# Ordering a kernel's instructions by another estimate of time: a transformer trunk, RWKV and S5 on one core

## The chip, the cores and the metric

The kernel runs on one core of a Trainium2 chip. The metric is device time in microseconds (us) of one execution. The engines are PE (TensorE, matrix products; PEld is its load of weights), DVE (VectorE), ACT (ScalarE), POOL (GpSimd) and SP, whose queue issues all transfers. Each engine takes the instructions of its queue in order and waits on semaphores for what other engines deliver.

## The reference

256 tokens of width 1024, with 256 tokens of context, pass two layers of a first block and one of a second, all in float32:

```
def first_block(x, c, ctx, ...):
    for l in range(2):
        mod, mod_c = silu(c) @ mod_w[l] + mod_b[l], silu(c_ctx) @ mod_w[l] + mod_b[l]
        x, xc = trunk_layer(x, xc, mod, mod_c, ...)
    return x

def trunk_layer(x, xc, mod, ...):
    z = split_columns((rmsnorm(x, pre_g) * (1 + scale) + shift) @ w_in)
    y_mla  = mla_branch(...)      # latent attention, 8 heads
    y_pool = pool_branch(...)     # mean over windows of 2, 4, 8, 16
    y_gla  = gla_branch(...)      # gated linear attention, 4 heads, both directions
    out = merge_branches(z, y_mla, y_pool, y_gla, w_branch_mla, w_branch_pool, w_branch_gla, w_out)
    return x + gate * rmsnorm(out, post_g), xc ...

def second_block(x, ...):
    proj = rms_norm(x, norm_mix_pre) @ w_in
    o_rwkv = rwkv7_branch(...) @ w_branch_rwkv
    o_s5 = s5_branch(...) @ w_branch_s5
    mixed = (g_rwkv * o_rwkv + g_s5 * o_s5) @ w_out
    x = x + rms_norm(mixed, norm_mix_post)
    return x + rms_norm(conv_ffn(rms_norm(x, norm_ffn_pre), ...), norm_ffn_post)
```

## The kernel before, in words

Features lie on the 128 partitions and tokens along the free axis: 512 columns for context and tokens together in layer 0, 256 for the tokens alone in most of layer 1 and in the second block. Weights come as units of 128x2048 in the order of use, each in two halves (`unit`, L405; seven buffers named `raw`). A half is split into a high part on ACT (`wh`, L425) and a remainder on DVE or, for every fourth, on POOL (`wl`, L427), with four buffers each; `mm3` (L435) then makes three products for each block of weights, wh by the high part of the activations, wh by their remainder, wl by the high part (L442).

The Python program writes latency-bound chains and column products interleaved by hand: `weave` (L571) emits the steps of a chain and spreads the steps of a filler over them. Layer 0 and layer 1 weave the gated linear attention (44 steps; in each of 4 heads 8 levels, `plv` products at L1113, fed by multiplications of DVE and POOL at L1104 to L1107) with merges and pooling. The norm of a head's output takes token sums (`ps_ss`, L461, of the squares of L1131), a square root of small DVE instructions (`rsqrt`, L489 to L497) and a broadcast on PE (`ps_rb`, L469). The second block weaves the RWKV chain (14 + 10 + 11 steps) with the S5 and with gates and merges; `collect`, `boundary` and `enter` make the sums and norms between blocks. Then come the feed-forward (`pup`, `pdn`) and the end.

What the program writes is not yet the order of the queues. When the tile context closes, the framework's scheduler plays the whole program on a simulated machine. Whenever an engine comes free there, it issues, of the instructions of that engine that are ready on that machine and whose buffers are free, the one that was written first. The order that results is fixed in the queues. So the estimate of durations decides where an instruction stands, but the set of instructions, their engines, buffers and transfers are those of the program. In the emitted program of the kernel before, 1822 of 8768 products on PE stand ahead of one that was written earlier, and so do 1097 of 2224 instructions on DVE, 519 of 1189 on ACT, 199 of 499 on POOL and 57 of 424 transfers on SP. At a few places the program adds an edge to hold an order (`issue_after` in `mod_chunk` and `update_x`).

Of the kernel before, what the change touches and what calls it, by code (L numbers as in the profile page):

```python
# [15 lines left out]
ALU = mybir.AluOpType  # L16
# [3 lines left out]
L = 256  # L20
# [9 lines left out]
TAU = 16.0  # L30
NSLOT = 62
MOD_AT = (0, 1, 4)     # input tiles ahead of which the next columns of the first modulation are made
S5_EARLY = 13          # state tiles of the S5 that go with the columns of the RWKV


# ---------------------------------------------------------------- host side layout
# [14 lines left out]
def _rope():  # L51
    cos, sin = _rope_tables()
    tab = np.ones((P, 2, L), np.float32)
    tab[64:96, 1], tab[96:128, 1] = cos, sin * ROPE_SIGN[:, None]
    tab[96:128, 0] = 0.0
    tab = tab.reshape(P, 2 * L)
    return np.stack([tab, np.concatenate([tab[64:], tab[:64]])])      # even heads, odd heads


class Layout:  # L60
    """Offsets of named blocks inside one [128, n] array."""
# [24 lines left out]
def _constants():  # L86
# [20 lines left out]
    sg[:64, 0], sg[64:, 0] = -1 / TAU, 1 / TAU     # decay sign of a key towards the state  # L107
    sg[:64, 1], sg[64:, 1] = 1 / TAU, 0.0
    sg[:64, 2], sg[64:, 2] = 1 / TAU, -1 / TAU     # decay sign of a query from the state
# [22 lines left out]
def _constants2():  # L132
    """tables of the second block, four [128, 512] pieces"""
# [24 lines left out]
def _w_tile(w, cols):  # L158
    """[K, len(cols)] block of w as [128, K/128 * len(cols)] (k tile major)."""
    b = w[:, cols]  # L160
    k = b.shape[0]
    return np.ascontiguousarray(b.reshape(k // P, P, -1).transpose(1, 0, 2)).reshape(P, -1)
# [18 lines left out]
def mod_columns(ch):  # L181
    """two groups of 256 columns of mod_w: chunks 0..3 shift and scale of two feature tiles, 4 and 5 halves of the gate"""
# [3 lines left out]
def host_unit(inp, key):  # L186
    """One [128, 2048] unit of the weight stream."""
# [103 lines left out]
def gate_weights(inp, l):  # L291
    """decay gates of the linear attention, on the partitions of their low-rank inputs"""
# [6 lines left out]
# ---------------------------------------------------------------- device side  # L299
# [5 lines left out]
class Halves:  # L305
    """a unit of the weight stream in two tiles, sliced like one [128, 2048]"""
# [10 lines left out]
class Arena:  # L317
    """[128, 512] slots, handed out as float32 or float32r tiles"""
# [18 lines left out]
    def cols(self, n):  # L337
        """[128, n] float32 (n = 512 or 256); two of 256 share a slot"""
# [21 lines left out]
class B:  # L360
# [43 lines left out]
    # -- weights  # L404
# [16 lines left out]
    def split(self, src, n, pool=False):  # L421
        """exact high part and remainder of a [128, n] block of weights"""
# [12 lines left out]
    def mm3(self, ps, w, xs, cols, off=0, m=P, start=True, stop=True):  # L435
        """ps += W.T @ X over len(xs) contraction tiles, with split operands"""
# [8 lines left out]
    # -- small helpers  # L445
    def after(self, ts, value):
        """[128, 1] constant that exists once the (finite) tiles ts do: keeps activations of one table together"""
# [7 lines left out]
    def token_sums(self, ps, c0, *accs, f=None):  # L455
        """ps[:, c0 + t] = f * sum over the partitions of token tile t of accs; returns the next column"""
# [8 lines left out]
    def bcast(self, r, n, pool):  # L465
        """PSUM [128, 128 n]: per-token columns r spread over all partitions"""
# [10 lines left out]
    def rstd(self, acc, dim, pool):  # L477
        """PSUM broadcast of 1/sqrt(mean + eps) from sums of squares that are still spread over partitions"""
# [4 lines left out]
    def rsqrt(self, m, n):  # L483
        """m ** -0.5 of a small tile: bit estimate, then a second- and a third-order step"""
# [7 lines left out]
        nc.vector.scalar_tensor_tensor(r, t, -3.0, r, ALU.add, ALU.mult)      # -2 times the second estimate  # L492
# [7 lines left out]
    # -- residual stream: x += out * rstd(out), then the next block's normalised input  # L500
    def collect(self, st, ps, gain, xs, nxt=True):
        """take one output tile: keep it times its gain and add up the sums the norms need"""
# [26 lines left out]
        if k == 6:  # L529
            # the sums of all tiles but the last, ahead of it  # L530
# [11 lines left out]
    def boundary(self, st, A, n, nxt=True):  # L542
        """PSUM broadcasts of rstd(out) and of rstd(x + out * rstd(out)); A: mean square of x per token, plus eps"""
# [27 lines left out]
def weave(chain, nc_, filler, nf):  # L571
    """emit a latency-bound chain (nc_ steps) with filler work (nf steps) spread over it"""
# [9 lines left out]
def mix(a, c):  # L582
    """step two generators in turn until the first ends, then finish the second"""
# [7 lines left out]
def mod_chunk(b, l, ch, ahead=False, between=None):  # L591
    """mod_columns(ch) of silu(c) @ mod_w + mod_b for (c_ctx, c)"""
# [35 lines left out]
def build_h(b, k, xs, seqs, gain, shift, pr2, hi_, lo_):  # L628
    """normalised (and modulated) input tile k, as its high part and remainder"""
# [15 lines left out]
def update_x(b, k, st, xs, s_, pr, rs, on_pool):  # L645
    """x += out * rstd; rs: copy of pr in SBUF, for the tiles of the engine that can't read PSUM"""
# [12 lines left out]
def enter(b, st, xs, s_, A, h, gain, shift, pool):  # L659
    """residual of one sequence, then its normalised input of the next block into h, tile after tile"""  # L660
# [11 lines left out]
def trunk(b, l, xs, st, A):  # L672
    """one layer of the first block; st: output tiles of the layer before that x still lacks"""
# [3 lines left out]
    QC = ALLC if full else XC          # columns that get an output  # L677
# [5 lines left out]
    # ---- pre norm, and the first columns as its tiles come  # L683
# [94 lines left out]
    def mla_prep():  # L778
# [12 lines left out]
        # rotary keys for the cosine and the sine part of the queries, on the lower and the upper partitions  # L791
# [25 lines left out]
    def parts(t):  # L817
        """a [128, 512] slot as its high part and remainder, in two new ones"""
# [5 lines left out]
    # ---- attention  # L824
# [40 lines left out]
    def pair_values(hd, prs, vt, py):  # L865
        """both heads of a pair, one product of each in turn: they fall on different columns of the array"""
# [23 lines left out]
    def silu2(ps):  # L890
        """2 * silu of a PSUM tile"""
# [1180 lines left out]
```

## Time and profile before

| | |
|---|---|
| median of 3 runs | 1586.6 us (1584.66 to 1589.52) |
| span of the profiled execution | 1585.3 us |
| its time with what lies around the span | not shown apart; span and median differ by 1.3 us |
| PE, PEld, DVE, ACT, POOL busy | 91%, 78%, 70%, 43%, 31% |
| moved from and to HBM | 188.19 MB, 119 GB/s on the mean |

An engine's busy time is the time that its instructions cover. Products on PE overlap each other, so a busy PE isn't one at its peak; idle time is what lies between. The granted clock of PE is a mean over its two levels, 1.00 for 2.4 GHz throughout and 0.50 for 1.2 GHz.

### The profile page before, as it was taken

The numbers are of one execution on the slowest core, as the hardware profiler recorded it, in microseconds if no ns is written. First come the engines' busy times: TensorE is split into PE (matmuls) and PEld (weight loads), VectorE is DVE, ScalarE is ACT, GpSimd is POOL, SyncE is SP. The second block draws the span as 40 slices with busy tenths as digits, with TensorE's granted clock in tenths as the row PEclk, the third lists the DMA queues.
The fourth block names the chain that finished last, engine by engine and source line by source line (L and its number), as shares of the span: only waits on it lengthen the run. The fifth ranks groups of instructions, "written<-read, shape, count | busy, mean of one in ns | idle before, by whom it ended". The sixth has DMA issues, their size and how long they took to land. (4 is left out here: it accounts for less than half of the span.)

```text
span 1585.3 us, 26747 instructions
## 1 busy us (share of the span) xinstructions
PE 1448.5 (91%) x10316; PEld 1232.7 (78%) x10316; DVE 1116.2 (70%) x2224; ACT 684.7 (43%) x1251; POOL 490.5 (31%) x503
## 2 busy tenths in 40 slices
PE   5999999998999999899988899979879999699997
PEld 2676766876788778886777799867548998699996
DVE  4565558886768655865599977779987348888843
ACT  3434445333323334354554445532343235366642
POOL 1000013353335954410134421436541002521212
PEclk8999999999999999899999999979989999799999
DMA  9634421221133262234033245834103224356550
GB/s 354 206 115 150 134 93 40 92 71 51 55 94 110 76 224 88 94 107 160 27 91 109 81 136 171 272 100 127 51 24 94 69 81 145 95 174 188 184 182 32
DMA packets 61183, 188.19 MB, mean 119 GB/s; under 512 B 7040, under 2 KB 8448, under 8 KB 61056
## 3 DMA queue, kind: packets, MB, share of 16 engines
q1 hardware_dynamic: 61056, 186.49, 36.7%
q8 instruction: 81, 1.33, 0.3%
q14 instruction: 46, 0.38, 0.1%
HBM read 180.43 MB, written 6.03 MB: 118 GB/s over the span
## 5 line engine op out<-in xcount | busy, mean ns | idle before, releaser
L425 ACT CAST wh<-raw 128x1024 fp32r<-128x1024 f32 (+1 forms) x296 | 279.6, 949 | 308.0 <-issue 64.5
L427 DVE TENSOR_TENSOR wl<-raw,wh 128x1024 fp32r<-128x1024 f32 (+1 forms) x225 | 271.2, 1208 | 162.8 <-ACT wh L425 159.8
L427 POOL TENSOR_TENSOR wl<-raw,wh 128x1024 fp32r<-128x1024 f32 (+1 forms) x71 | 144.2, 2032 | 649.0 <-ACT wh L425 600.1
L442 PE MATMUL z_merge<-s,wh 128*128 128x512 f32 (+1 forms) x768 | 198.7, 347 | 1.3 <-ACT s L940 1.3
L442 PEld LDWEIGHTS z_merge<-s,wh 128*128 128x128 f32 x768 | 134.0, 194 | 17.7 <-issue 2.0
L442 PE MATMUL z_merge<-s,wl 128*128 128x512 f32 (+1 forms) x384 | 131.8, 343 | 2.2 <-DVE wl L427 2.1
L442 PE MATMUL pbr<-s,wh 128*128 128x256 f32 (+1 forms) x512 | 120.2, 325 | 3.5 <-ACT s L432 2.4
L442 PE MATMUL pup<-s,wh 128*128 128x256 f32 x656 | 118.5, 283 | 0.1
L442 PEld LDWEIGHTS pup<-s,wh 128*128 128x128 f32 x656 | 102.5, 192 | 0.2 <-ACT wh L425 0.2
L442 PE MATMUL y<-s,wh 128*128 128x256 f32 x496 | 98.7, 294 | 0.0
L442 PE MATMUL pwo<-s,wh 128*128 128x256 f32 (+1 forms) x448 | 95.3, 310 | 2.7 <-ACT s L1220 2.0
L442 PEld LDWEIGHTS pbr<-s,wh 128*128 128x128 f32 x512 | 86.2, 191 | 12.8 <-ACT s L432 3.0
L442 PE MATMUL pup<-s,wl 128*128 128x256 f32 x328 | 92.8, 283 | 0.0
L442 PEld LDWEIGHTS z_merge<-s,wl 128*128 128x128 f32 x384 | 74.5, 194 | 11.5 <-DVE wl L427 3.2
L442 PE MATMUL pbr<-s,wl 128*128 128x256 f32 (+1 forms) x256 | 83.1, 325 | 0.0
L442 PEld LDWEIGHTS y<-s,wh 128*128 128x128 f32 x496 | 78.6, 193 | 5.8 <-issue 3.5
L442 PEld LDWEIGHTS pwo<-s,wh 128*128 128x128 f32 x448 | 76.0, 202 | 6.6 <-ACT s L1220 2.6
L1102 ACT ACTIVATE s<-s 128x512 f32<-128x512 f32 (+1 forms) x64 | 33.1, 523 | 97.2 <-DVE s L1101 92.6
L442 PE MATMUL y<-s,wl 128*128 128x256 f32 x248 | 71.6, 289 | 2.2 <-DVE wl L427 2.2
L432 ACT CAST s<-s 128x256 fp32r<-128x256 f32 (+1 forms) x88 | 42.8, 488 | 69.1 <-DVE s L1175 19.6
L442 PE MATMUL pwo<-s,wl 128*128 128x256 f32 (+1 forms) x224 | 69.0, 308 | 1.5 <-DVE wl L427 1.5
L1113 PE MATMUL plv<-s,s 128*128 128x128 f32 x384 | 53.9, 284 | 14.4 <-POOL s L1105 8.2
(478 smaller groups left out, 3684.9 us busy)
## 6 DMA issues: line engine op xcount, KB each, us to landing
raw<-wts SPq DMA_DIRECT2D x294, 512.0 KB, 4.3
s<-wts SPq DMA_DIRECT2D x57, 256.0 KB, 5.4
s5t<-s SPq DMA_DIRECT2D x16, 256.0 KB, 2.0
s<-s5t SPq DMA_DIRECT2D x16, 256.0 KB, 3.4
s<-xc SPq DMA_DIRECT2D x8, 256.0 KB, 4.0
x<-xc SPq DMA_DIRECT2D x8, 256.0 KB, 4.8
s<-tabs SPq DMA_DIRECT2D x4, 256.0 KB, 4.6
out<-s SPq DMA_DIRECT2D x8, 128.0 KB, 1.8
```

Source lines behind the costliest of these rows:

```text
L425: self.nc.scalar.copy(hi[:, :n], src)
L427: self.last_lo = eng.tensor_sub(lo[:, :n], src, hi[:, :n])
L432: self.nc.scalar.copy(hi, src)
L442: self.nc.tensor.matmul(ps, u, v[:, cols], start=start and n == 0, stop=stop and n == last)
L1102: nc.scalar.activation(E[:, lo:], E[:, lo:], AF.Exp, scale=1.0 / TAU)
L1113: nc.tensor.matmul(ps[:, c], K_[:, j], Z[:, c], start=True, stop=True)
```

## The change

The tile context gets the flag by which the scheduler plays the program on the framework's timeline simulation, with that simulation's durations, instead of on its plain estimate. All else of the program is the same; the other lines of the diff take comments away and leave the line numbers.

```
--- before.py
+++ after.py
@@ -2057,7 +2057,7 @@
     ap["wts"] = nc.dram_tensor("wts", (n_units, P, UNIT), F32, kind="ExternalInput").ap()
     ap["out"] = nc.dram_tensor("out", (8, P, L), F32, kind="ExternalOutput").ap()
-    with tile.TileContext(nc) as tc:
+    with tile.TileContext(nc, schedule_with_timeline_sim=True) as tc:
         b = build(tc, ap, lay)
         assert len(b.order) == n_units, len(b.order)
```

## Rows read from the trace of the kernel before

**Rows 1.** The page: busy us, share of the span, instructions of three engines.

```profile
PE 1448.5 (91%) x10316; PEld 1232.7 (78%) x10316; DVE 1116.2 (70%) x2224; ACT 684.7 (43%) x1251; POOL 490.5 (31%) x503
```

**Rows 2.** Busy time by stage: stretch, length, engines, granted clock, DMA share, GB/s.

```profile
0.00:40.00 40.00, 23.21 (x78) 8.72 (x81) 18.70 (x46) 14.44 (x28) 5.13 (x6) 0.83 0.96 351
40.00:240.00 200.00, 196.45 (x1062) 137.79 (x1062) 113.19 (x336) 87.30 (x180) 13.41 (x13) 1.00 0.42 138
240.00:600.00 360.00, 338.62 (x1647) 276.84 (x1646) 268.36 (x448) 134.31 (x213) 175.17 (x199) 0.99 0.29 93
600.00:800.00 200.00, 186.58 (x1214) 156.69 (x1213) 129.17 (x302) 92.09 (x188) 50.99 (x57) 0.95 0.28 91
800.00:920.00 120.00, 100.38 (x729) 94.88 (x728) 112.31 (x286) 61.76 (x125) 51.90 (x73) 0.93 0.31 93
920.00:1000.00 80.00, 80.00 (x661) 79.80 (x660) 56.13 (x99) 38.89 (x65) 14.58 (x14) 0.98 0.55 173
1000.00:1043.00 43.00, 31.10 (x217) 29.72 (x216) 31.32 (x57) 18.41 (x36) 25.12 (x25) 0.79 0.68 224
1043.00:1200.00 157.00, 135.63 (x997) 102.65 (x998) 140.13 (x220) 63.38 (x118) 74.71 (x66) 0.92 0.23 73
1200.00:1320.00 120.00, 117.12 (x1802) 109.07 (x1797) 59.12 (x123) 37.45 (x75) 8.78 (x6) 0.99 0.28 85
1320.00:1393.00 73.00, 58.81 (x438) 56.69 (x436) 60.19 (x112) 34.96 (x67) 28.14 (x27) 0.86 0.39 116
1393.00:1573.00 180.00, 179.56 (x1493) 179.10 (x1492) 120.36 (x182) 101.21 (x160) 39.38 (x16) 1.00 0.52 161
1573.00:1585.30 12.30, 1.01 (x6) 0.71 (x6) 7.27 (x23) 0.48 (x2) 3.17 (x4) 0.70 0.25 85
```

**Rows 3.** Waits of PE from 240 to 600: total us, times, longest.

```profile
PE plv L1113 <- POOL s L1105: 8.2, 5, 2.2
...
PE z_merge L442 <- DVE wl L427: 2.1, 1, 2.1
PE pbr L442 <- ACT s L432: 2.0, 1, 2.0
PE ps_ss L461 <- ACT s L1131: 1.8, 1, 1.8
```

**Rows 4.** Instructions in order of time around 379 us: start, duration, engine.

```profile
377.64 0.42 DVE L1106 TENSOR_TENSOR s<-s,s 64x256 f32<-64x256 f32 x1
377.65 1.11 POOL L1104 TENSOR_TENSOR s<-s,s 64x256 f32<-64x256 f32 x1 [2.44 <-ACT s L1102]
...
378.10 0.94 DVE L1107 TENSOR_TENSOR s<-s,s 64x256 f32<-64x256 f32 x1
378.72 1.01 POOL L1105 TENSOR_TENSOR s<-s,s 64x256 f32<-64x256 f32 x1
...
379.78 1.16 PE L1113 MATMUL plv<-s,s 128*128 128x128 f32 x8 [1.71 <-POOL s L1105]
...
383.60 0.71 PE L442 MATMUL z_pool_gate<-s,wh 128*128 128x512 f32 x2
```

**Rows 5.** The same view from 1102 to 1112 us, DVE, then PE.

```profile
1102.56 1.21 DVE L427 TENSOR_TENSOR wl<-raw,wh 128x1024 fp32r<-128x1024 f32 x1
1103.69 0.17 DVE L490 TENSOR_TENSOR t<-r 128x16 f32<-128x16 f32 x1
1103.78 0.68 DVE L1551 TENSOR_TENSOR s<-bu,s 128x512 f32<-128x512 f32 x1
...
1109.18 1.17 DVE L497 SCALAR_TENSOR_TENSOR r<-u,r 128x16 f32<-128x16 f32 x1
...
1111.10 1.46 PE L1532 MATMUL py<-s,s 128*32 128x256 f32 x3 [3.11 <-DVE rnk L1635]
```

**Rows 6.** The chain that ended last: the feed-forward's first product.

```profile
1393.17 115.42 PE pup L442 x960
```

More of the change, by code (lines that the diff above doesn't have):

```diff
@@ L2059, in make @@
     ap["out"] = nc.dram_tensor("out", (8, P, L), F32, kind="ExternalOutput").ap()
-    with tile.TileContext(nc) as tc:
+    with tile.TileContext(nc, schedule_with_timeline_sim=True) as tc:
         b = build(tc, ap, lay)
```

## The prediction

> **What bounds the kernel now.** I read four views: the shares of the engines, the busy time by stage, the waits of the matrix engine, and the order of time around a few of its gaps.
>
> The shares say that the matrix engine (PE) leads with 1448.5 us of a span of 1585.3, before DVE with 1116.2 and POOL with 490.5 [rows 1]. So an order of instructions can win back only the 1585.3 - 1448.5 = 136.8 us in which PE is idle, and what a low clock costs in its busy time. The stages show where these lie [rows 2]. Idle time is the length less PE's busy time; clock loss is the length times what the granted clock lacks to 1.00 (a mean over 1.2 and 2.4 GHz).
>
> - 0 to 40: 16.8 idle, while the DMA engines are busy for 0.96 of the time: the first weights arrive.
> - 40 to 240, 920 to 1000, 1200 to 1320: 3.6, 0 and 2.9 idle. Nearly full.
> - 240 to 600 (attention chain of layer 0): 21.4 idle, 3.6 of clock.
> - 600 to 800 (end of layer 0, start of layer 1): 13.4 and 10.0.
> - 800 to 920 (the same chain in layer 1): 19.6 and 8.4; DVE is busy for 112.3 of 120 us.
> - 1000 to 1043 and 1320 to 1393: 11.9 and 14.2, the two block boundaries.
> - 1043 to 1200 (RWKV chain and S5): 21.4 and 12.6; DVE is busy for 140.1 of 157.
> - from 1393: 11.7 idle, all but 0.4 of it in the last 12 us; before that 960 products of the feed-forward follow each other in 115.42 us [rows 6], 0.120 us each, with no gap to fill.
>
> **The change part by part.** It removes and adds no instruction, transfer or byte. It replaces the estimate by which the scheduler decides what is ready when an engine comes free. The queues run in order, so a wrong estimate costs in two ways: an instruction stands too early and its engine waits in front of ready work, or ready work of lesser urgency goes first and the chain waits.
>
> The first kind is in the trace. At 379.78 PE has waited 1.71 us for POOL's product of L1105, which took 1.01 us after one of 1.11 [rows 4]; the column products behind it start at 383.60 without a wait. The order before treats POOL as if it were done by then. Between 240 and 600 such waits for POOL come to 8.2 us, and 1.8 more for the square of L1131 [rows 3]. The waits of 2.1 and 2.0 us for a weight split and for the inputs of the merge [rows 3] have no other work behind them and stay.
>
> The second kind is there too: in the square root of the RWKV norms every small DVE instruction stands behind a large one, 0.17 us (L490) after a split of 1.21, and so on to L497 at 1109.18; PE then waits 3.11 us [rows 5]. An order by another estimate can mend this or spread it.
>
> An estimate nearer to the chip should mostly shorten waits of the first kind. No row shows the new order, so each stage is bounded by nothing gained and by all of its idle and clock time:
>
> - 240 to 600: waits with work behind them 8.2 + 1.8 = 10.0, clock 3.6. Two thirds of the first and half of the second: 9 us (bounds 0 and 13.6). I take most here because DVE is busy for only 268 of 360 us, so PE sets the end of the stage.
> - 600 to 800: a third of 13.4 + 10.0: 8 us (0 and 23.4). DVE at 129 of 200 leaves room, but part of this is the boundary between the layers, with little to put in.
> - 800 to 920: a quarter of 28.0: 7 us (0 and 28.0). DVE at 94% is nearly a second bound; work pulled into a gap is missing at the end of the stage, where PE then waits for the chain.
> - 1043 to 1200: an eighth of 34.0: 4 us (0 and 34.0), for the same reason.
> - Beginning, two boundaries and end: 0. Their 54.6 us of idle are a transfer or chains of sums and norms with no columns left; the order among a few dependent instructions has nothing to exchange.
> - Feed-forward and 920 to 1000: 0. PE is full, and its columns depend on nothing late.
>
> That is 28 us. Against it stand the stages where the present order leaves PE hardly idle. 40 to 240 and 1200 to 1320 mix chains with columns as 240 to 600 does, and idle 6.4 us of 320; at the rate of 240 to 600, 21.4 of 360, it would be 19.0. A new order can only lose here, 0 to 12.6 us. I take two thirds, 8, since nothing says that the new order hits the same lucky places. SP's queue moves too, in the sense that its loads are ordered by the same estimate: the 16.8 us at the start bound it, and elsewhere the DMA engines are at most 0.68 busy [rows 2], so I cost it at 0; were that cover gone, a late load would hold a split and then PE, as at the start.
>
> **A rule against the change.** DVE and POOL lengthen each other: L1106 on DVE took 0.42 us as POOL's L1104 began, and the like-shaped L1107, wholly beside it and its successor, 0.94 [rows 4]. A better packed order has more such pairs. 64 levels run in the attention chains (2 layers of 4 heads of 8 levels). One more lengthened DVE instruction in each costs 0.5 us in layer 0 and, on half the columns, 0.25 in layer 1: 16 + 8 = 24 us, of which only the 8 of layer 1 surely reach the end, since DVE has 92 us free between 240 and 600. The Trainium skill, "GPSIMD Engine Reference", section Key points, states that GpSimd shares its SBUF interfaces with VectorE and contends with instructions that have two SBUF inputs, and the trace agrees (0.42 against 0.94). By the page alone the sum would lose these 8 to 24 us; I leave them out of the sum, because the pairs exist already and a new order may have fewer, and keep them as a rival.
>
> **The sum.** 28 - 8 = 20 us less. The profiled execution has a span of 1585.3 us, 1.3 below the median of 1586.6 and inside the runs shown (1584.66 to 1589.52); what lies around the span isn't shown apart, and I carry the 1.3 over. 1585.3 + 1.3 - 20 = 1566.6, so 1567.
>
> **The rivals.**
>
> *The chains swallow it.* Where DVE is busy for 94 and 89%, filling PE's gaps only moves the idle time to the end of the stage, and 600 to 800 is boundary. Then 9 us are won and 8 lost: 1586. For it: DVE's two near-full stages hold half of the idle time that order could reach. Against it: in 240 to 600 PE is the later one.
>
> *Fillers overtake the chains (slower).* Place: DVE's queue from 800 to 920 and 1043 to 1200, with 44 steps of one chain and 35 of the other as the kernel weaves them. Price: a weight split of 1.21 us [rows 5] started just before a chain instruction is ready delays it by half on the mean, 0.6. Half of the 79 steps hit cost 24 us; the 11 us of these stages aren't won, so 9 + 8 - 8 = 9 remain as gain: 1586.6 + 24 - 9 = 1602. It decides from 15 steps on (9 / 0.6). For it: rows 5 show the pattern already, and the order before puts chains early, which costs PE but protects them. Against it: a split that goes early isn't there later, and a chain that PE no longer blocks starts sooner.
>
> *Closer pairing of DVE and POOL*, as above: 1567 + 8 to 24, 1575 to 1591, middle 1583.
>
> *Larger gain.* Half of all that order could reach: (13.6 + 23.4 + 28.0 + 34.0) / 2 = 49.5, nothing lost: 1537. For it: most of those waits have columns behind them. Against it: DVE's share.
>
> The change does nothing at all only if both estimates agree on every choice; rows 4 show the old one off by more than a microsecond, so I give that no chance of its own.
>
> **How the numbers follow.** Forecast 0.48 (own range 1547 to 1583: 28 us give or take 12, the loss between 0 and 12.6), swallowed 0.16, overtaken 0.22, pairing 0.06, larger 0.08. A measurement of this kernel tells 0.3%, 4.8 us, from no change: faster is below 1581.8, slower above 1591.4. Faster: 0.47 of the forecast and 0.08, 0.55. Same: swallowed and the rest of the forecast, 0.17. Slower: overtaken, and pairing as far as losses join it, 0.28. The range must take in both signs: 1540 leaves out half of the larger gain (0.04), 1610 the worse third of overtaken (two thirds of the 79 steps cost 32 us: 1610) and a little else, 0.10.
>
> **What the new profile would show.** Right: PE's busy share above 91%; waits of L1113 for POOL under 4 us in the attention stage of layer 0; that stage shorter by some 9 us and the one after it by some 8; the feed-forward still at 0.120 us a product, the boundaries still with 12 and 14 us idle. Swallowed: the waits for POOL gone, but the stage as long, with a wait at its end. Overtaken: fewer waits of PE in the middle of columns, but long ones for DVE, and splits ahead of small instructions on DVE. Pairing: the mean duration of the same DVE instructions up. I'd be wrong altogether if new gaps opened in the stages that are now full, or if loads of weights came late.

## The result and the profile after

The changed kernel took 1644.45 us in the median (1643.18 to 1645.43), the kernel before beside it 1585.84 (1584.66 to 1589.52): a ratio of 1.0367, 95% interval 1.0344 to 1.0390. It is slower by 58 us; the prediction was faster by 20. The instructions are the same; only their order in the five queues differs.

The page of the profile after, with the busy time of the engines, answers to [rows 1]:

```profile
PE 1457.9 (89%) x10316; PEld 1238.5 (75%) x10316; DVE 1121.7 (68%) x2224; ACT 683.9 (42%) x1251; POOL 506.4 (31%) x503
```

The span is 1642.8 us, so PE is idle for 184.9 us where it was idle for 136.8. The mean granted clock fell from 0.956 to 0.937 of full speed (a mean over 1.2 and 2.4 GHz): 1642.8 x 0.063 = 103.5 us lost, 1585.3 x 0.044 = 69.8 before. But for part of the time at the low clock PE is idle anyway, and that part must not be counted twice. Counted along the clock records of the trace, with half of the busy time at 1.2 GHz as lost, the low clock takes 67.2 us out of PE's busy time, 51.4 before. What is left, PE's work at full clock, went down from 1397.1 to 1390.7. So idle time added 48.1 us, the clock 15.8, and shorter work took 6.4 away: 57.5 in all, the difference of the spans.

Busy time by stage, to be set against [rows 2]. The borders are put by the same products: the first `pgate` product, where the linear attention starts, moved from 239 to 280, the first `pwo` from 586 to 608, the last `pgate` from 798 to 843, the first of the second block from 1042 to 1081.

```profile
40.00:281.00 241.00, 218.65 (x1122) 153.85 (x1121) 114.88 (x342) 91.61 (x184) 13.53 (x13) 0.95 0.35 116
281.00:621.00 340.00, 324.90 (x1606) 267.62 (x1606) 274.81 (x447) 131.95 (x210) 185.15 (x200) 0.99 0.29 92
621.00:846.00 225.00, 197.79 (x1305) 165.92 (x1305) 133.42 (x308) 97.52 (x195) 51.73 (x58) 0.92 0.27 91
846.00:1038.00 192.00, 166.89 (x1294) 160.67 (x1293) 165.64 (x377) 94.68 (x182) 66.69 (x86) 0.95 0.40 126
1038.00:1082.00 44.00, 29.18 (x216) 27.92 (x215) 33.49 (x64) 17.74 (x37) 26.74 (x25) 0.80 0.64 225
1082.00:1255.00 173.00, 150.00 (x1074) 115.04 (x1074) 146.51 (x223) 65.60 (x121) 79.15 (x66) 0.86 0.26 79
1255.00:1371.00 116.00, 110.07 (x1736) 103.43 (x1735) 49.92 (x109) 33.99 (x69) 6.42 (x5) 0.93 0.23 71
1371.00:1451.00 80.00, 58.12 (x421) 54.73 (x421) 59.92 (x117) 34.91 (x67) 30.71 (x27) 0.85 0.32 100
```

Worked out as in the prediction (idle is length less PE's busy time, the clock's loss is length times what the clock, rounded to two digits, lacks to 1.00); the column after it is the loss in PE's busy time alone, from the clock records:

| stage (before) | length | PE idle | lost to the clock | in busy time alone | forecast |
|---|---|---|---|---|---|
| 40 to 240, latent attention of layer 0 | 200 -> 241 | 3.6 -> 22.4 | 0 -> 12.1 | 0 -> 10.6 | part of +8 |
| 240 to 600, linear attention of layer 0 | 360 -> 340 | 21.4 -> 15.1 | 3.6 -> 3.4 | 5.1 -> 1.7 | -9 |
| 600 to 800, with the latent attention of layer 1 | 200 -> 225 | 13.4 -> 27.2 | 10.0 -> 18.0 | 9.9 -> 13.7 | -8 |
| 800 to 1000, linear attention of layer 1 | 200 -> 192 | 19.6 -> 25.1 | 10.0 -> 9.6 | 9.9 -> 6.6 | -7 |
| 1043 to 1200, RWKV and S5 | 157 -> 173 | 21.4 -> 23.0 | 12.6 -> 24.2 | 9.2 -> 15.9 | -4 |
| 1200 to 1320, RWKV and merges | 120 -> 116 | 2.9 -> 5.9 | 1.2 -> 8.1 | 1.7 -> 7.6 | part of +8 |
| 1320 to 1393, boundary | 73 -> 80 | 14.2 -> 21.9 | 10.2 -> 12.0 | 5.4 -> 4.9 | 0 |

A stage can also grow or shrink because columns are done ahead of it; the experiments take that apart. Two terms came as forecast. The feed-forward's products follow each other as in [rows 6]:

```profile
1450.90 115.42 PE pup L442 x960
```

And PE no longer waits for POOL in the linear attention of layer 0. These waits of PE from 280 to 608 are all there are in the place of [rows 3]:

```profile
PE plv L1113 <- DVE s L1116: 5.6, 7, 1.4
PE pst L1075 <- ACT s L1073: 3.3, 1, 3.3
PE pbr L442 <- ACT s L432: 2.0, 1, 2.0
PE ps_rb L469 <- DVE r L497: 1.5, 1, 1.5
PE po L1125 <- DVE s L1116: 1.4, 2, 0.9
PE plv L1113 <- DVE s L1107: 0.8, 1, 0.8
PE pst L1072 <- DVE s L1068: 0.3, 1, 0.3
```

**Where the loss begins.** In the latent attention a chain (`mla_chain`, L911) makes for each of 8 heads the keys and queries (`pk`, `pq`), the scores (`psc`, L851), their softmax on DVE and ACT (L853 to L858), the transposes (`ptr`, L876) and the values (`py`, L883). It is woven at L1206 with filler columns that don't depend on it: the gates, the first columns of the linear attention (`pgv`, L1016) and the next modulations (`pmod`, L606). PE's waits from 105 to 280 in the kernel after:

```profile
PE psc L851 <- ACT s L432: 5.8, 4, 3.0
PE psc L851 <- ACT s L856: 5.7, 4, 1.4
PE ptr L876 <- ACT s L856: 3.5, 5, 1.7
PE pq L442 <- ACT s L856: 1.7, 1, 1.7
PE pmod L614 <- ACT s L612: 1.1, 2, 0.7
PE psc L851 <- DVE s L433: 1.1, 2, 0.6
```

In the same stage of the kernel before, PE waited 0.8 us for the scores' operands, once, and 0.7 for others. One such place in the changed kernel, in order of time (start, duration; in brackets PE's or ACT's idle time and what ended it):

```profile
156.56 0.28 PE L1016 MATMUL pgv<-wl,s 128*128 128x256 f32 x1
...
165.46 1.66 PE L442 MATMUL pq<-s,s 128*128 128x512 f32 x6
168.46 1.04 ACT L425 CAST wh<-raw 128x1024 fp32r<-128x1024 f32 x1 [0.93 <-DMA raw<-wts]
170.08 0.90 PE L851 MATMUL psc<-s,s 128*128 128x256 f32 x4 [2.95 <-ACT s L432]
...
173.76 2.91 PE L851 MATMUL psc<-s,s 128*128 128x512 f32 x6
176.47 0.63 PE L1016 MATMUL pgv<-wh,s 128*128 128x256 f32 x2
```

Between the query and the scores PE has nothing else to do: the last column product ended at 156.8 and a modulation at 163, and the weights of the next columns have only arrived at 168.46. Their loads had waited for a buffer that a modulation product on PE still had to read, as the longest of the waits of SP's queue from 140 to 175 shows:

```profile
SPq L410 <- PE pmod L606: 21.6, 1, 21.6
```

In the kernel before, such products of a query and its scores had column products between them (a query at 121.77, columns from 123.28 on, the scores at 124.89). The busy time of the stretches around the place shows that the clock falls too; the number after the engines is the granted clock:

```profile
140.00:160.00 20.00, 16.44 (x107) 12.68 (x107) 8.86 (x29) 8.41 (x20) 0.00 (x0) 1.00 0.39 141
160.00:180.00 20.00, 16.61 (x85) 11.57 (x83) 10.04 (x27) 8.65 (x18) 2.52 (x1) 0.83 0.47 157
180.00:200.00 20.00, 16.74 (x81) 11.55 (x84) 6.05 (x18) 7.44 (x18) 0.00 (x0) 0.74 0.00 1
```

PE idles for 3.6 us in the first stretch at full clock, and then runs at a mean of 0.83 and 0.74. The six score products above took 2.91 us; the like six took 1.66 in the kernel before.

How far the fillers run ahead can be counted along PE's instructions in their order: the filler products that stand ahead of the first score product of each head of layer 0.

| head | 1 | 2 | 3 | 4 | 5 | 6 | 7 | 8 |
|---|---|---|---|---|---|---|---|---|
| before | 101 | 130 | 165 | 207 | 265 | 301 | 353 | 408 |
| after | 148 | 196 | 232 | 260 | 348 | 400 | 404 | 408 |

There are 408, so the last three heads have almost none left. From these rows came the first theory: the fillers overtake the chain in PE's queue, which costs the 62 us by which the two latent-attention stages grew up to their `pgate` products (in layer 0 139.4 to 175.0 us from 100 and 105 on, in layer 1 119.3 to 145.8 from the last `z_misc` product on). The rivals: the weight loads come late; or the queues of DVE and ACT hold the chain up.

### The profile page after: what moved, and what is told of

Same layout as the page of the kernel before. It is cut to its first block, busy times and chain, and to the rows that moved or that the text cites. A ratio compares the mean times of both kernels' runs of the same rounds, so it can differ in the third digit from the quotient of the medians.

```text
span 1642.8 us, 26795 instructions
## 1 busy us (share of the span) xinstructions
PE 1457.9 (89%) x10316; PEld 1238.5 (75%) x10316; DVE 1121.7 (68%) x2224; ACT 683.9 (42%) x1251; POOL 506.4 (31%) x503
## 4 chain that ended last, share of the span: by engine, by line
PE 40%; DVE 12%; issue 2%; ACT 2%; POOL 1%; DMA 1%; DVEq 0%; ACTq 0%; POOLq 0%
PE pup L442 7%; PE y L442 5%; PE pdn L442 4%; PE z_merge L442 3%; PE pbr L442 3%; DVE wl L427 2%; PE py L1532 2%; PE pgv L1016 1%; PE pwo L442 1%; PE pen L442 1%; DVE s L1520 1%; PE py L883 1%; DMA raw<-wts 1%; PE z_mla_gate L442 1%; PE z_gla_gate L442 1%
## 5 line engine op out<-in xcount | busy, mean ns | idle before, releaser
L427 POOL TENSOR_TENSOR wl<-raw,wh 128x1024 fp32r<-128x1024 f32 (+1 forms) x71 | 148.8, 2097 | 740.9 <-ACT wh L425 662.2
L442 PE MATMUL z_merge<-s,wh 128*128 128x512 f32 (+1 forms) x768 | 194.8, 341 | 2.4 <-ACT s L940 1.3
L442 PE MATMUL pbr<-s,wh 128*128 128x256 f32 (+1 forms) x512 | 125.7, 332 | 3.5 <-ACT s L432 2.0
L442 PE MATMUL pwo<-s,wh 128*128 128x256 f32 (+1 forms) x448 | 89.6, 299 | 0.0
L433 DVE TENSOR_TENSOR s<-s,s 128x256 fp32r<-128x256 f32 (+1 forms) x88 | 51.9, 593 | 37.3 <-ACT s L432 34.7
L442 PEld LDWEIGHTS pwo<-s,wh 128*128 128x128 f32 x448 | 72.0, 191 | 2.6
L1113 PE MATMUL plv<-s,s 128*128 128x128 f32 x384 | 56.8, 290 | 18.9 <-DVE s L1116 12.0
L1113 PEld LDWEIGHTS plv<-s,s 128*128 128x128 f32 x384 | 51.2, 200 | 25.9 <-issue 16.1
```

The source lines that it names most:

```text
L427: self.last_lo = eng.tensor_sub(lo[:, :n], src, hi[:, :n])
L433: self.nc.vector.tensor_sub(lo, src, hi)
L442: self.nc.tensor.matmul(ps, u, v[:, cols], start=start and n == 0, stop=stop and n == last)
L1113: nc.tensor.matmul(ps[:, c], K_[:, j], Z[:, c], start=True, stop=True)
```

## The experiments

### Whose order is it?

An order can be copied. Every instruction has the same name in both kernels, so a list of names in the order of one kernel, with an edge from each to the next that fixes the order in the queue and waits for nothing, gives a chosen queue in a chosen stage of the other kernel that order (the edits are shown in outline here and below):

```diff
         b = build(tc, ap, lay)
+        for names in ORDERS.values():     # per engine, in the order to be copied
+            for last, name in zip(names, names[1:]):
+                tc.add_manual_dep(named[name], last, edge)   # order alone, no wait
```

What is on no list is left to the scheduler. **pe_order_old** lists PE in the two latent-attention stages.

> The changed kernel, with one thing put back: in the two latent-attention stages the matrix engine's queue has the order that it had before the change; the other queues and all other stages stay with the timeline estimate. Theory (on PE's queue the filler columns overtake the attention chain, so that the chain is late and its end has no columns left): the 62 us by which the two stages grew (35.6 and 26.5) come back for the most part, 1575 to 1605 us, and PE's idle time and its low clock in them go. Rival 1 (weights arrive late because the load queue was reordered): no more than 10 us come back, above 1630. Rival 2 (DVE's and ACT's queues hold the chain up): half or less, above 1610.

1617.2 us, ratio to before 1.0198 (1.0180 to 1.0216): 27 us came back, not 40 to 70. That lies outside the theory's bounds and inside those of rival 2, which the next run tests.

**dve_act_order_old** lists DVE, ACT and POOL there instead.

> The changed kernel, with DVE's, ACT's and POOL's queues in the two latent-attention stages in the order before the change, PE's and the load queue free. Rival 2 (those queues hold the chain up): 1575 to 1605. Theory (PE's queue does it): these queues alone bring back less than half of the 62 us, 1610 to 1650, since PE still sends the fillers ahead of the chain (196 filler products lie ahead of the second head's first score product, 130 in the kernel before; here 172).

1655.9 us, 1.0443 (1.0424 to 1.0462): nothing came back; it is 12 us slower than the changed kernel.

**load_order_old** lists SP's queue, in the whole program.

> The changed kernel, with the load queue of the whole program in the order before the change and all else free. Rival 1 (late loads): 1600 or less. Theory: no change, 1638 to 1650, since a load waits for its buffer, and the buffers are freed by PE's and DVE's order.

1652.9 us, 1.0429 (1.0413 to 1.0444): nothing came back, 8 us slower. So the order of the loads isn't what makes the weights late; at the place above they waited for a buffer that PE had to free.

**pe_order_new_alone** is the reverse, in the kernel before.

> The reverse, in the kernel before: only PE's queue in the two latent-attention stages gets the order of the changed kernel, all else goes by the plain estimate. Theory (that order alone makes the loss): 40 to 65 us more than before, 1626 to 1651. If the loss needs the other queues too (rival 2) or the loads (rival 1): less than 20 us more, below 1606.

1621.4 us, 1.0235 (1.0216 to 1.0253): 35 us lost by PE's order in these two stages alone, a little less than the theory's least. Where, the starts of the same products show. The last column before the forms is first and last start, of the kernel before and of this one:

```profile
L1027 PE MATMUL pgate<-s,s x16: 587/587/692, 239.4 to 797.7; 32*128 32x512 f32 x16
L442 PE MATMUL pwo<-s,wh x448: 277/283/561, 586.5 to 1360.0; 128*128 128x256 f32 x128, 128*128 128x512 f32 x22
L442 PE MATMUL pup<-s,wh x656: 280/283/415, 1380.0 to 1508.2; 128*128 128x256 f32 x164
```

```profile
L1027 PE MATMUL pgate<-s,s x16: 587/587/692, 267.8 to 836.3; 32*128 32x512 f32 x16
L442 PE MATMUL pwo<-s,wh x448: 277/283/561, 612.8 to 1393.3; 128*128 128x256 f32 x128, 128*128 128x512 f32 x22
L442 PE MATMUL pup<-s,wh x656: 280/283/415, 1413.3 to 1541.2; 128*128 128x256 f32 x164
```

28.4 us are lost by the first `pgate`, 26.3 by the first `pwo` of layer 0, 38.6 by the last `pgate`, 33.3 by the feed-forward; nothing is lost after the stages whose order was changed.

**mla_all_old** lists all five queues in the two stages.

> The changed kernel, with all five queues in the two latent-attention stages in the order before the change. If PE's order alone matters there: as with PE's alone, 1613 to 1620. If the other queues' orders matter together with PE's: 5 to 20 us less, 1597 to 1612; what is left above 1586 is then the RWKV stage's loss (19 us) less the gain in the linear-attention stages.

1615.6 us, 1.0182 (1.0167 to 1.0197): as with PE's alone. In these stages the order of the other queues adds nothing to that of PE, which is worth 27 us taken back and 35 put in. The theory had the right queue and stage and half the size: the 62 us were measured up to the `pgate` products, and part of them was work done ahead. With all five old orders the first `pgate` still starts at 263.6, 24.2 later than before, but the first `pwo` at 591.1, only 4.6 later. 29 us stand elsewhere.

### Is it the lead of the fillers?

**fillers_held** keeps the timeline estimate and holds the fillers by the step:

```diff
     for _ in chain:
         i += 1
+        ends.append(last PE product traced so far)
+        with b.tc.issue_after(ends[-2]):       # from the second step on
             while done * nc_ < i * nf and next(filler, 1) is None:
                 done += 1
```

> The changed kernel, with a rule in place of a copied order: in the two latent-attention stages the PE products of a filler step are queued behind the last PE product of the chain step before the one after which they are written, so a filler can be at most about one step ahead. Theory (it is the lead of the fillers over the chain that costs, not this or that detail of the order): as much comes back as with PE's whole old order, 20 to 35 us, 1610 to 1625. Rival (other details of PE's order make the loss): less than 10 us back, above 1635.

1637.3 us, 1.0318 (1.0301 to 1.0336): 7 us back, within the rival's bounds. The filler products ahead of the heads' first scores are now 108, 132, 168, 180, 240, 288, 348 and 360, fewer than before the change from the fourth head on, and still PE waits. The largest of its waits from 104 to 269 in this kernel (total, times, longest):

```profile
PE psc L859 <- ACT s L864: 13.1, 8, 3.0
```

(L859 and L864 are L851 and L856.) The lead is gone from the fourth head on and the loss in layer 0 is not: the first `pwo` starts at 607.2, in the changed kernel at 607.7.

**fillers_rationed** spreads them: filler product n goes behind the chain product at the same share of the chain as product n - 60 has of the fillers (never behind one that is written after it); **fillers_rationed_40** and **fillers_rationed_80** change the 60.

```diff
+        for n, ins in enumerate(filler products):
+            m = (n - 60) * len(chain products) // len(filler products)
+            tc.add_manual_dep(ins, chain products[m], edge)
```

> The changed kernel, with the filler products of the two latent-attention stages rationed on PE: product n of the fillers is queued behind the chain product that stands at the same share of the chain as product n - 60 does of the fillers, so the stock is spread over the chain's waits and no step can use it up in its first wait. Theory (holding fillers by the step gave nothing back in layer 0 since a step's stock is spent in its first wait; spread, it covers all waits): as with PE's old order, 15 to 30 us less than the changed kernel, 1614 to 1630. Rival (some other detail of PE's old order is what counts): less than 8 us, above 1636.

1628.9 us, 1.0268 (1.0240 to 1.0295): 15 us back.

> fillers_rationed with an allowance of 40 products in place of 60. Theory (spreading the fillers over the chain's waits gives back part of what PE's order cost): 10 us or more under the changed kernel, below 1634. Rival (the 15 us that came back with 60 are scatter, since any change of the order moves the time by some 10 us either way, as it did for the loads' order, +8, and the late fillers, +12): anywhere within 8 us of the changed kernel, 1636 to 1652.

1639.9 us, 1.0328 (1.0303 to 1.0353): 5 us back, within the rival's bounds.

> fillers_rationed with an allowance of 80. Theory: less than with 60 comes back, 4 to 16 us, 1628 to 1640. Rival (scatter): as likely slower as faster than the changed kernel.

1631.2 us, 1.0278 (1.0252 to 1.0304): 13 us back.

**chain_24_forward** leaves the fillers in their lumps and moves the chain up:

```diff
+        for each chain product: ahead = max(ahead - 24, fillers written before it)
```

> The changed kernel, PE's queue in the two latent-attention stages in its own new order, but with each chain product moved up past as many as 24 filler products that were written after it; the fillers keep their lumps. If the lead as such costs: 8 us or more come back, below 1636. If it matters how the fillers lie among the chain's waits, and not how far ahead they are: within 8 us of the changed kernel, 1636 to 1652.

1646.8 us, 1.0381 (1.0355 to 1.0408): no change. This run alone is a weak test, since the lead of the changed kernel over the one before is 47 to 99 products for the first seven heads, and 24 take away only part of it.

So the lead as such, held in fillers_held and cut in chain_24_forward, doesn't explain the loss. A ration, which is meant to put a few filler products into each wait, gave 5, 15 and 13 us back, always with the sign of the theory and never the 27 of the old order; with orders that were expected to change nothing or to help (loads, and DVE with ACT and POOL) moving the time by 8 and 12 us, only part of this is safe. That the fillers must lie between the chain's waits is supported, not shown; what makes the rest of the 27 us stays open.

**fillers_early** and **fillers_early_half** go the other way, in the kernel before with its plain estimate:

```diff
+        with b.tc.high_priority(240):          # 120 in fillers_early_half, -80 in fillers_late
             while done * nc_ < i * nf and next(filler, 1) is None:
```

> The kernel before with its plain estimate, where the filler steps of the two latent-attention stages are given the priority of instructions written 240 places earlier, so that they run as far ahead of the chain as in the changed kernel (196, 260, 400, 408 filler products ahead of the first score products of heads 2, 4, 6 and 8 of layer 0; 130, 207, 301, 408 in the kernel before). Theory (the lead costs): 25 to 45 us more than before, 1611 to 1631, as with the copied order of PE. Rival (the timeline estimate's order is bad for another reason): within 10 us of before, below 1596.

1666.8 us, 1.0508 (1.0486 to 1.0530): 80 us lost, more than expected. PE idles 39.3 us longer than before (1665.3 - 1489.2 = 176.1), the clock takes 19.3 more of its busy time, and the work at full clock is 21.4 longer.

> As fillers_early, the plain estimate with the fillers of the two latent-attention stages written early, but by 120 places and not 240 (169, 260, 338, 408 filler products ahead of the first score products of heads 2, 4, 6 and 8; 130, 207, 301, 408 before, 196, 260, 400, 408 with 240, which cost 80 us). Theory (the loss grows with the lead, and faster once the stock runs out): 10 to 40 us more than before, 1597 to 1627. Rival (the loss is all in the start, where fillers pushed the chain back by 27 us): proportional there alone, under 10 us, below 1597.

1615.0 us, 1.0180 (1.0150 to 1.0210): 29 us lost, as expected, but not in the way expected: PE's busy time is 1476.9 of a span of 1616.2 at a mean clock of 0.954, so it idles for 139.3 us, hardly more than the 136.8 before. The work itself is longer by 26.0 us, and the last section shows the most of why. So of these two only the first bears the theory out, and a quarter of its loss (21.4 of 80) is longer work.

> The kernel before with its plain estimate, the filler steps of the two latent-attention stages written 80 places later (57, 151, 238, 355 filler products ahead of the first score products of heads 2, 4, 6 and 8; 130, 207, 301, 408 before). Theory (only fillers that run ahead cost): within 8 us of before, 1579 to 1595, since fillers that are left over are done in the next stage. Rival (the order before is a point to which the steps were fitted, and any departure from it costs): 12 us more or over, above 1599.

1598.1 us, 1.0073 (1.0047 to 1.0099), 12 us more, between the two bounds. PE idles less than before (1597.6 - 1465.9 = 131.7), its work is longer by 15.2. So late fillers don't make PE wait, but this departure from the old order costs too, by the same lengthening of the work.

### The other half

**rwkv_new_alone**: all queues listed in the old order up to the second block, free under the timeline estimate from there.

> The timeline estimate with all queues in the old order up to the start of the second block, and free from there. If the RWKV stage's loss stands by itself: 14 to 24 us over before, 1600 to 1611, and then the loss of the change is the sum of this, of the 33 to 35 us of PE's order in the latent-attention stages and of about nothing elsewhere. Rival (it comes with the state that the first block leaves in the queues): below 1595.

1607.4 us, 1.0129 (1.0098 to 1.0159): 20 us (16 to 25) lost in the second block alone. The busy times by part, first of the kernel before and then of this one, cut at the start of the block, the last input product of the S5 (`bu`) and at the end of the RWKV's first score products (`sc`):

```profile
1042.00:1153.00 111.00, 101.20 (x640) 77.47 (x640) 99.46 (x153) 43.28 (x76) 56.76 (x51) 0.94 0.30 93
1153.00:1197.00 44.00, 32.10 (x296) 23.06 (x297) 38.68 (x63) 18.56 (x40) 18.88 (x17) 0.84 0.06 17
1197.00:1380.00 183.00, 166.05 (x2205) 156.07 (x2201) 113.49 (x221) 68.77 (x135) 36.69 (x32) 0.94 0.34 104
```

```profile
1045.00:1143.00 98.00, 92.11 (x614) 72.28 (x616) 89.39 (x132) 35.80 (x62) 51.79 (x44) 0.97 0.33 104
1143.00:1211.00 68.00, 50.03 (x426) 37.41 (x424) 54.85 (x88) 30.11 (x61) 28.27 (x23) 0.80 0.16 48
1211.00:1394.00 183.00, 155.73 (x2101) 145.91 (x2097) 105.33 (x216) 63.52 (x127) 36.20 (x31) 0.91 0.30 91
```

The S5, which is the filler there, ends 13 us sooner, and the stretch from there to the end of the first score products takes 24 us longer, with 18.0 us idle for 11.9 and a clock of 0.80 for 0.84. But 130 more products run in it, most of them taken from the third stretch, which then idles for 27.3 us for 17.0 at the same length. So the block loses idle time after the S5's end and more of it later on; which instruction stands wrong is not shown. The profiled execution is the fastest of its four, and its block is only 11 us longer.

**rwkv_dve_old** (DVE's queue of the second block in the old order, all else of the changed kernel) and **pe_order_old_and_rwkv** (pe_order_old, with PE's queue of the weaves at L1934 to L1937 as well) ask which queue it is.

> The changed kernel, with DVE's queue in the second block up to the feed-forward's start (RWKV chain, S5, merges) in the order before the change, all else free. Theory (there the S5's instructions overtake the RWKV chain in DVE's queue: 59 of them lie ahead of the first broadcast of the key norms, 39 before the change): 10 to 20 us come back, 1624 to 1634. Rival (the loss there is on PE, or comes with the state that the first block leaves): less than 5 us, above 1639.

1644.4 us, 1.0360 (1.0342 to 1.0378): no change.

> pe_order_old with PE's queue in the RWKV stage's weaves (RWKV chain, S5, merges) in the old order as well. If the RWKV stage's loss of 17 us is PE's order too: 1598 to 1606. If it is not (DVE's order alone gave nothing back): 1612 to 1622.

1633.4 us, 1.0294 (1.0266 to 1.0323): 16 us slower than without it. Neither of these two old orders mends it, and an old order in one queue beside new ones in the others can do harm of its own.

**rwkv_fillers_early** puts the fillers of the four weaves 80 places earlier, under the plain estimate.

> The kernel before with its plain estimate, the filler steps of the second block's four weaves (S5 steps, merge columns) written 80 places earlier. PE's queue then has 60 S5 products ahead of the first broadcast of the key norms and 444 merge products ahead of the last (44 and 407 before; 61 and 444 in the changed kernel). Theory (the same mechanism as in the latent-attention stages): 12 to 50 us more than before, 1599 to 1637, lost from the S5's end on. Rival (the RWKV stage loses in another way): below 1595.

1761.6 us, 1.1119 (1.1075 to 1.1163): 176 us, far outside, and by another mechanism (last section).

**timeline_for_gla_only** lists all queues in the old order except from the linear attention to the end of each layer.

> The timeline estimate with all queues in the old order everywhere but from the linear-attention stage of each layer to the layer's end, so that the estimate is free only where the trace seemed to show a gain (the stage was 19 us shorter in layer 0 and 7 in layer 1). If that gain is real: 1565 to 1580, better than both kernels. If it was only columns done ahead in the stage before it: 1582 to 1592, no change.

1589.8 us, 1.0021 (1.0006 to 1.0036): no gain that lasts. The first `pwo` starts at 581.2, 5.3 us sooner than before, and the first product of the second block at 1042.5, 0.2 later. Layer 0 gains and layer 1 gives it back.

Where the loss stands, the starts of the same products show (first `pwo` in layer 0, first `bu` in the second block, first `pup` of the feed-forward, from their tiles' views):

| | first `pwo` | first `bu` | first `pup` |
|---|---|---|---|
| before | 586.5 | 1060.1 | 1380.0 |
| after | 607.7 | 1097.5 | 1438.1 |
| mla_all_old | 591.1 | 1069.0 | 1407.9 |
| pe_order_new_alone | 612.8 | 1093.2 | 1413.3 |
| rwkv_new_alone | 589.9 | 1061.0 | 1394.4 |

The change loses 37.4 us up to the first `bu`, and the old orders of the latent attention bring 28.5 of them back; it loses 20.7 us from there to the first `pup`, and they change that little (19.0). Put into the kernel before, the parts are 35 us (PE's order in the latent attention), 20 (second block) and 3 (linear attention to the end of the layers), 58 together; that this meets the whole so closely is in part luck, since PE's order gave back only 27 when it was taken out. No kernel that ran beat the one before.

## Why the prediction was wrong

- **PE bounds the kernel, and order can only move its idle time and clock.** PE leads after the change too. But the prediction read the bound in one direction: 136.8 us to win. Nothing bounds the loss, since an order can make idle time where there was none.
- **Waits for POOL go (right).** 8.2 us before, no row after. In their place stand 5.6 us for L1116 on DVE.
- **240 to 600 gains 9 us (mechanism right, size off).** The stage is 20 us shorter, but 13.7 of it are PE's busy time for 41 products fewer, done outside the stage; idle time fell by 6.3. By itself (timeline_for_gla_only) the new order there gained 5 us by the first `pwo`, and they were lost again by the second block.
- **800 to 920 gains 7 (wrong).** Shorter by 8 with the columns after it, but its idle time rose (19.6 to 25.1), and in timeline_for_gla_only layer 1 lost what layer 0 had won.
- **The step that failed: "A new order can only lose here, 0 to 12.6 us", put at 8.** The nearly full stages were priced at the idle rate of another stage. Instead, PE's new order in the two latent-attention stages cost 35 us by itself (pe_order_new_alone). In the changed kernel PE's idle time rose by 18.8 us in 40 to 240, and by another 13.8 in 600 to 800, which holds the latent attention of layer 1 and was counted as a gain of 8. The idle rate of 240 to 600 is no bound for a stage with other waits: there are eight heads here, each with a softmax between two groups of products, and PE's waits in the first of the two stages rose from 1.5 us to 18.9. The prediction named the sign itself ("if new gaps opened in the stages that are now full") and gave it no price beyond 12.6.
- **What the clock adds.** The prediction counted the clock as something to win, never as a price of a new order. Up to the first `bu` this matters little: 35.7 us more of idle time, 2.5 of clock in busy time, 0.8 less work make the 37.4. From there to the first `pup` it is the larger part: 12.1 of idle time, 13.9 of clock, 5.3 less work make the 20.7.
- **1043 to 1200 gains 4 (wrong).** The second block alone lost 20 (rwkv_new_alone). It stays open which queue does it.
- **SP's queue costs nothing (right as far as tried).** Its old order gave nothing back. The boundary put at 0 at 1320 was not: it idles 7.7 us longer.
- **The rival that came nearest** was "Fillers overtake the chains", with the right sign, but it was placed on DVE in the linear attention and the RWKV stage; the largest part is on PE in the latent attention, where none of the rivals looked. In the place that it named, DVE's old order in the second block gave nothing back (rwkv_dve_old). That the S5 runs ahead there and the chain ends later is in line with it, but no run isolates it. In the latent attention the number of fillers ahead explains little by itself.
- **Closer pairing of DVE and POOL** is hardly seen: the 128 instructions of L1104 to L1107 on DVE take 66.2 us, 63.7 before. The pair read for it was ill-chosen, since L1106 with its 0.42 us ran beside POOL's L1104 for nearly all of its time too [rows 4]. The trace of the kernel before bears the lengthening out as a whole: of the 16 instructions of L1107 on 64x256, the three with no POOL beside them took 0.42 us, and the nine that ran beside it for nearly all or all of their time had a median of 0.84.
- **Two sums.** Idle time and clock loss of a stage were added to one bound (34.0 from 1043 to 1200), though part of the low clock lies in the idle time: in that stage only 9.2 us of the clock's loss fall in busy time. And pairing was counted with the slower outcomes, though its own range, 1575 to 1591, ends below the 1591.4 from which a time counted as slower. Neither changes the sign of the forecast.

Why an estimate that removes the waits for POOL makes a worse order: the scheduler has no goal, it takes what is ready. Argued, not shown: on an estimate with longer latencies PE comes free in more of the chain's waits, and the fillers are spent in the first of them.

## What to carry to other kernels

A greedy scheduler's estimate is part of the program that was laid out by it: a change of the estimate is a change of every queue, and stages without idle time are where it can only lose. Price such a change by the stages that are full, not by the waits it would mend. And to find the queue at fault, copy one queue's order at a time, in both directions, and keep in mind that a mixture of orders can cost something by itself (8 to 16 us here).

## What the runs showed of the hardware

**Idle time and a low clock overlap.** Span times mean clock makes the changed kernel's clock loss 33.7 us larger, but only 15.8 of it lie in PE's busy time; the rest lies in time that is idle already. A sum of idle time and such a clock loss counts that rest twice.

**PE's work depends on what stands next to what.** The modulation products use 32 columns of the array and the small RWKV products a quarter of it. Together they are fast: in the changed kernel, and for the small ones, behind column products, in the kernel before,

```profile
127.03 1.92 PE L606 MATMUL pmod<-raw,sc 128*32 128x512 f32 x16
```

```profile
1226.41 0.28 PE L442 MATMUL y<-s,wl 128*128 128x256 f32 x1
1226.62 1.15 PE L1753 MATMUL pQ<-s,s 64*64 64x64 f32 x32
```

Of the sixteen, four start within 0.02 us of each other, and the next four 0.43 to 0.45 us later. In fillers_early_half the products of the norm's sums come between them (L607 is L606):

```profile
105.21 1.05 PE L607 MATMUL pmod<-raw,sc 128*32 128x512 f32 x2
106.18 0.38 PE L461 MATMUL ps_ss<-cons,s 128*128 128x1 f32 x2
106.50 1.04 PE L607 MATMUL pmod<-raw,sc 128*32 128x512 f32 x2
```

Two and two take 1.29 us (106.50 - 105.21), where two of sixteen took 0.24: the two modulation products start 0.45 us apart, one after the other and not side by side. In rwkv_fillers_early column products and pairs of small ones alternate (L1754 is L1753):

```profile
1302.47 0.58 PE L442 MATMUL y<-s,wh 128*128 128x256 f32 x1
1302.98 0.47 PE L1754 MATMUL pQ<-s,s 64*64 64x64 f32 x2
1303.38 0.58 PE L442 MATMUL y<-s,wh 128*128 128x256 f32 x1
```

0.91 us for one column product and two small ones, at a granted clock of 0.50; by the rows of the kernel before, each among its own kind, they take 0.12 + 0.07 us at full clock, which would be an estimated 0.38 at half. The Trainium skill, "TensorEngine Tiling (Array Packing)", section Key Properties, states that changing the tiling mode drains the engine; these rows agree. The price of one change at full clock is small: in the kernel before, a column product of 128x256 is followed by the next after 0.12 us and by a small product after 0.21 (1226.62 - 1226.41), as in the median of 4950 and of 32 such pairs.

Counted along PE's instructions, the tile shape changes from one product to the next 268 times in fillers_held, 271 in the changed kernel, 290 before, 307 in fillers_late and 328 in fillers_early_half, and PE's work at full clock is 1379.4, 1390.7, 1397.1, 1412.3 and 1423.1 us. At 0.09 us the 60 changes between the ends are an estimated 5 of the 43.7 us. More goes with the modulations: their 192 narrow products start in 66, 70, 88, 100 and 112 groups, and a group is followed by the next after 0.43 us or more, whether it has one product or four, so 46 more groups are an estimated 20 us. The rest isn't taken apart, and there is no one price for a change: rwkv_fillers_early has 711 and works 1463.0 us.

**The clock can fall while PE counts as busy all the time.** In rwkv_fillers_early, where such products alternate:

```profile
1240.00:1280.00 40.00, 40.00 (x427) 30.73 (x425) 8.63 (x11) 5.38 (x9) 0.00 (x0) 0.80 0.14 41
1280.00:1320.00 40.00, 40.00 (x213) 27.45 (x213) 3.29 (x4) 3.69 (x6) 1.27 (x1) 0.54 0.04 14
1360.00:1400.00 40.00, 40.00 (x276) 29.75 (x277) 5.76 (x19) 4.81 (x14) 1.26 (x1) 0.50 0.05 14
```

0.50 is 1.2 GHz throughout. The run idles for 1755.4 - 1608.1 = 147.3 us, 10.5 more than before, but loses 145.2 us of its busy time to the clock, for 51.4, and its work is 65.9 longer. A busy share of 100% is no sign that the engine is well used.
